# Turning k, q, v and the output of a gated delta rule by VectorE block transposes and DMA, with v's tile ahead of q's

## The chip, the cores and the metric

The kernel runs on one core of one Trainium2 chip. The metric is the device time of one launch in microseconds (us), the median of several runs. The core has five engines with queues of their own: TensorE (PE; its weight loads are listed as PEld), VectorE (DVE), ScalarE (ACT), GpSimd (POOL) and SyncE (SP), which here only issues DMAs. Sixteen DMA engines move the data.

## What is computed

The reference is one step of a decoder layer, in float32, for 512 new prompt tokens and 8 sample tokens of width 2048. The part that matters here is the gated delta rule of the prompt, with 8 heads of width 128. Its kernel form works on chunks of 128 tokens, four to a head.

```
xn  = rmsnorm(h);  proj = xn @ w_in            # q | k | v | z | beta | decay | pool
qkv = silu(short_conv(proj_qkv))               # 4 taps along the tokens
q, k = l2norm(q) * 128**-0.5, l2norm(k)
...
u  = solve(I + strict(k k^T * beta * decay), v * beta)     # and w, from k
qk = tril(q k^T * decay)
for each chunk:                                # the chain through the state S
    v_new = u - w S
    o = (q * exp(g)) S + qk v_new
    S = S * exp(g_last) + k_dec^T v_new
out = rmsnorm(o, dn_norm) * silu(z)
```

After that come a pooling group, the output projection, and a SwiGLU block, none of which the change touches.

## The kernel before, in words

All activations lie with channels on the 128 partitions and tokens along the free dimension: 8 sample columns and 512 prompt columns. A projection tile is 128 columns of the weights by all tokens. `product` (L172) makes it out of 16 k-steps, each of six matmuls (L168 to L170: two halves of the tokens, by three passes over the high and low parts of weights and activations). The weights come in granules of eight k-steps: SP loads `raw` (L131), ScalarE cuts off the high part (`hi`, L135), VectorE the rest (`lo`, L137), each in three buffers. These three carry a raised priority.

The stage of the change is the first one, up to L1163. For each half of the heads (0 to 3, then 4 to 7) the loop at L1101 makes the four k tiles, then four z tiles (L1111), then for each head the q tile and the v tile (`qv_tiles`, L1089). `qkv_tile` (L730) evicts the product into `ext` (L259, VectorE), runs four convolution steps (L737, L739) and SiLU on ScalarE (L740).

The delta rule's own small matmuls are woven into the products: `Weave` (L43) holds generators in two tracks, `product` calls `weave.step()` once per k-step, and a generator's `yield n` asks for n steps until its next piece. A task may be added with a delay in steps. TensorE's instructions stay in the order in which the program writes them (L522); those of the other engines and of SP are put in order by a scheduler that ranks ready instructions by their place in the program, raised for the weights and the evictions.

- `keys(h)` (L760) runs in track 1, 16 steps behind its k tile: k k^T (L766), the four transposes of k (L769) into PSUM, their squares on ScalarE (L757), the row factors, `nn` (L781) and the decayed keys `kd` (L783). The diagonal blocks of `nn` go through DRAM to `eliminate` (L794), 62 short VectorE instructions that invert them for four heads at a time; the result comes back as `utf` (L1093).
- `delta(h, qT, vT)` (L817) runs in track 0, from one step behind the second of the head's two tiles: the product with the inverse (L831), four transposes of q (L838) and their squares, two steps later L850 and the product of k and q (L857), then four transposes of v (L865) scaled into `vs` (L867), then the chain over the chunks (L877 to L896) with R and S on VectorE and W on ScalarE (L886). At its end squares of the output give row factors, and L910 writes the scaled output over `nn`.
- `gate(h)` (L913), in track 1, 8 steps later: four transposes of the output (L916), and one VectorE instruction that multiplies by the norm's weight and the gate into the mixed activations (L918), which are read again at L1140, behind the pool tiles.

What a transpose serves: k, q, v and the output exist with channels on partitions, while row factors and the chain want tokens there. A transpose is a TensorE instruction with the identity as one operand, and its result lies in PSUM.

## Time and profile before

| | |
|---|---|
| median of 3 runs | 2160.74 us (2160.28 to 2161.4) |
| the profiled execution | span 2158.9 us from first to last instruction |
| TensorE busy | 2136.1 us, 99% of the span |
| VectorE busy | 1746.4 us, 81% |
| ScalarE busy | 929.6 us, 43% |
| GpSimd busy | 433.8 us, 20% |
| DMA | 297.04 MB, queue of SP and ScalarE 36.3% of 16 engines |
| granted TensorE clock | 0.999 |

The profile comes from one execution; its times are those of that execution, while the median is of runs without one. A line such as `L865 PE MATMUL dn<-ident,vT 128*128 128x128 f32 x32 | 4.9, 274` is a group of instructions: line of the kernel, engine, operation, tile written and tiles read, shape, count, then busy us in total and mean ns of one. In a timeline a row begins with its start and its length in us; x4 says that four instructions are merged in it; the bracket at its end gives the engine's idle time ahead of it and what ended that. The lengths of matmuls overlap, as they are pipelined. Names of buffers carry numbers now and then, which mean nothing.

### The profile page before, as it was taken

What the parts mean: (1) busy time and instruction counts of PE and PEld (TensorE: products, weight loads), DVE (VectorE), ACT (ScalarE), POOL (GpSimd) and SP (SyncE); (2) the same over time, 40 slices, a digit from 0 to 9 for tenths busy, and PEclk for the clock granted to TensorE, in tenths of its full rate; (3) what the DMA queues carried; (4) which work ended last, traced back from release to release, by engine and by line L of the source; (5) the groups of instructions that cost most, each with busy time, mean ns of one, the idle gap of its engine ahead of it and who ended that gap; (6) DMA issues with size and microseconds to landing.
All of it is one profiled execution on the core that took longest, in us unless ns stands there. A gap on an engine that the chain in (4) does not pass through costs nothing.

```text
span 2158.9 us, 42980 instructions
## 1 busy us (share of the span) xinstructions
PE 2136.1 (99%) x17809; PEld 2128.8 (99%) x17809; DVE 1746.4 (81%) x2619; ACT 929.6 (43%) x1404; POOL 433.8 (20%) x512
## 2 busy tenths in 40 slices
PE   8999999999999999999999999999999999999998
PEld 7999999999999999999999999999999999999998
DVE  7786667666499979988988888888877898887997
ACT  6533443432264545434433434434334444435444
POOL 2210110111012202233233233232113302003100
PEclk9999999999999999999999999999999999999999
DMA  8343234323445543554554454454446746438343
GB/s 281 92 110 91 76 94 112 88 76 96 120 121 161 152 119 111 155 166 141 145 166 139 147 167 143 142 163 134 125 147 189 234 111 205 115 103 247 93 108 119
DMA packets 442497, 297.04 MB, mean 138 GB/s; under 512 B 26556, under 2 KB 423253, under 8 KB 438957
## 3 DMA queue, kind: packets, MB, share of 16 engines
q1 hardware_dynamic: 422733, 219.94, 36.3%
q0 software_dynamic: 18256, 73.55, 10.5%
q8 instruction: 139, 2.28, 0.5%
q10 hardware_dynamic: 1312, 0.80, 0.1%
q14 instruction: 57, 0.47, 0.1%
HBM read 251.47 MB, written 43.43 MB: 137 GB/s over the span
## 4 chain that ended last, share of the span: by engine, by line
PE 86%; DVE 8%; DMA 2%; issue 2%; ACT 1%; POOL 1%; SPq 0%; DVEq 0%; POOLq 0%; ACTq 0%
PE dn L1223 20%; PE dn L1222 20%; PE dn L1224 20%; PE mm L168 6%; PE mm L170 6%; PE mm L169 6%; DVE lo L1216 2%; DVE raw L1244 1%; PE dn L850 1%; DMA st<-a_d 1%; DVE lo L137 1%; POOL st L1776 0%; DMA xt<-in_x_prompt_dram 0%; PE dn L960 0%; PE dn L857 0%
## 5 line engine op out<-in xcount | busy, mean ns | idle before, releaser
L1215 ACT CAST hi<-raw 128x1024 fp32r<-128x1024 f32 (+1 forms) x422 | 427.4, 1027 | 400.2 <-DVE raw L1244 206.5
L1216 DVE TENSOR_TENSOR lo<-raw,hi 128x1024 fp32r<-128x1024 f32 (+1 forms) x422 | 527.4, 1270 | 87.1 <-ACT hi L1215 85.6
L168 PE MATMUL mm<-xh,hi 128*128 128x256 f32 (+1 forms) x1280 | 379.7, 297 | 2.4 <-DVE mixa L259 2.4
L169 PE MATMUL mm<-xl,hi 128*128 128x256 f32 (+1 forms) x1280 | 361.5, 282 | 0.9 <-DVE xl L350 0.7
L170 PE MATMUL mm<-xh,lo 128*128 128x256 f32 (+1 forms) x1280 | 361.8, 283 | 0.4 <-DVE lo L137 0.4
L168 PEld LDWEIGHTS mm<-xh,hi 128*128 128x128 f32 x1280 | 241.4, 189 | 3.7 <-DVE mixa L259 3.1
L169 PEld LDWEIGHTS mm<-xl,hi 128*128 128x128 f32 x1280 | 241.7, 189 | 1.7 <-DVE xl L350 1.7
L170 PEld LDWEIGHTS mm<-xh,lo 128*128 128x128 f32 x1280 | 240.8, 188 | 0.6 <-DVE lo L137 0.6
L1244 DVE TENSOR_TENSOR raw<-raw 128x1024 f32<-128x1024 f32 (+1 forms) x130 | 175.3, 1349 | 2.2
L1223 PE MATMUL dn<-b21l,hi 128*128 128x260 f32 x620 | 175.7, 283 | 0.4 <-DVE b21l L1786 0.4
L1224 PE MATMUL dn<-b21h,lo 128*128 128x260 f32 x620 | 175.4, 283 | 0.0
L1222 PE MATMUL dn<-b21h,hi 128*128 128x260 f32 x620 | 175.0, 282 | 0.0
L1224 PE MATMUL dn<-b11h,lo 128*128 128x260 f32 x612 | 173.4, 283 | 1.2 <-DVE lo L1216 1.1
L1223 PE MATMUL dn<-b11l,hi 128*128 128x260 f32 x612 | 173.3, 283 | 0.0
L1222 PE MATMUL dn<-b11h,hi 128*128 128x260 f32 x612 | 172.7, 282 | 0.0
L1222 PE MATMUL dn<-T1h,hi 128*128 128x260 f32 x556 | 158.1, 284 | 0.0
L1223 PE MATMUL dn<-T1l,hi 128*128 128x260 f32 x556 | 157.7, 284 | 0.0
L1224 PE MATMUL dn<-T1h,lo 128*128 128x260 f32 x556 | 156.7, 282 | 0.0
L1222 PE MATMUL dn<-B22h,hi 128*128 128x260 f32 x548 | 155.9, 284 | 0.0
L1223 PE MATMUL dn<-B22l,hi 128*128 128x260 f32 x548 | 155.6, 284 | 0.0
L1224 PE MATMUL dn<-B22h,lo 128*128 128x260 f32 x548 | 154.6, 282 | 0.4 <-DVE lo L1216 0.4
L135 ACT CAST hi<-raw 128x1024 fp32r<-128x1024 f32 (+2 forms) x86 | 87.1, 1014 | 148.2 <-PE mm L169 139.4
(659 smaller groups left out, 6422.5 us busy)
## 6 DMA issues: line engine op xcount, KB each, us to landing
raw<-in_w_gate_up_dram SPq DMA_DIRECT2D x134, 512.0 KB
raw<-in_w_in_dram SPq DMA_DIRECT2D x79, 512.0 KB
a_d<-mixa POOLq DMA_DIRECT2D x22, 1040.0 KB, 5.5
raw<-in_w_down_dram SPq DMA_DIRECT2D x48, 448.0 KB
mixb<-in_w_gate_up_dram SPq DMA_DIRECT2D x41, 512.0 KB
raw<-in_w_out_dram SPq DMA_DIRECT2D x25, 512.0 KB
st<-a_d POOLq DMA_DIRECT2D x49, 260.0 KB, 6.5
raw<-in_w_down_dram SPq DMA_DIRECT2D x24, 512.0 KB
```

Source lines behind the costliest of these rows:

```text
L135: act.copy(hi[:, r], raw[:, r])
L137: dve.tensor_tensor(lo[:, r], raw[:, r], hi[:, r].bitcast(F32), op=ALU.subtract)
L168: te.matmul(acc[ci], wh, hi[k][:, c0:c1], start=(k == 0), stop=False)
L169: te.matmul(acc[ci], wh, lo[k][:, c0:c1], start=False, stop=False)
L170: te.matmul(acc[ci], wl, hi[k][:, c0:c1], start=False, stop=(k == len(w) - 1))
L850: te.matmul(yp[0:96, c, j], xt_[:, c, :], udf[:, c, j] if it == 0 else v3(cur)[:, c, j], start=True, stop=True)
L1215: act.copy(hi, raw)
L1216: dve.tensor_tensor(lo, raw, hi.bitcast(F32), op=ALU.subtract)
L1222: te.matmul(acc, wh[:, k, :], xf[:, k, :], start=start and k == 0, stop=False)
L1223: te.matmul(acc, wh[:, k, :], xg[:, k, :], start=False, stop=False)
L1224: te.matmul(acc, wl[:, k, :], xf[:, k, :], start=False, stop=stop and k == wh.shape[1] - 1)
L1244: dve.tensor_tensor(r[name], r[a], r[b], op=op)
```

## The change

A helper `turn_blocks` takes the place of the sixteen TensorE transposes of a head. VectorE transposes each 32x32 block of a [128, 512] tile into `bt`, one DMA writes `bt` to DRAM in rows of 128 numbers, and four DMAs read it back, each for 32 partitions, in pieces of 32 numbers, so that the blocks come to their transposed places. All five are issued by SP.

```diff
 BUFS:
-    "vs": 1
+    "vs": 2, "bt": 2, "tq": 1

+        tok_d = dram.tile([4, H, NCH, P, P], F32, name="tok_d")
+
+        def turn_blocks(kind, h, src, dst):
+            bt = d1tile("bt", [P, SEQ], "bt")
+            dve.transpose(bt, src)
+            d = tok_d[kind, h]
+            sp.dma_start(d.rearrange("c p f -> p c f"), v3(bt))
+            rows = d.rearrange("c (i p) (j q) -> j p (c i) q", p=32, q=32)
+            for j in range(4):
+                sp.dma_start(dst[32 * j:32 * j + 32, :].rearrange("p (n q) -> p n q", q=32), rows[j])

 keys:
-            kd = kds[h] = d1tile("kd", [P, SEQ], "kd")
+            kd = kds[h]
-            ktp = pst()
-            for c in range(NCH):
-                te.transpose(ktp[:, ck(c)], kT[:, ck(c)], ident)
-            squares(ktp, ss)
+            squares(kd, ss)
-            dve.tensor_tensor(v3(kd), v3(ktp), bc3(ad), op=ALU.mult)
+            dve.tensor_tensor(v3(kd), v3(kd), bc3(ad), op=ALU.mult)

 delta:
-        def delta(h, qT, vT):
+        def delta(h, qT, qk, vs):
-            qtp = pst()
-            for c in range(NCH):
-                te.transpose(qtp[:, ck(c)], qT[:, ck(c)], ident)
-            squares(qtp, ss)
+            squares(qk, ss)
-                    vtp = pst()
-                    for c in range(NCH):
-                        te.transpose(vtp[:, ck(c)], vT[:, ck(c)], ident)
-                    vs = d1tile("vs", [P, SEQ], "vs")
-                    dve.tensor_tensor(v3(vs), v3(vtp), bc3(ik), op=ALU.mult)
+                    dve.tensor_tensor(v3(vs), v3(vs), bc3(ik), op=ALU.mult)
-            weave.add(gate(h, on), 1, 8)
+            turn_blocks(3, h, on, on)
+            weave.add(gate(h, on), 1, 12)

 gate:
-            otp = pst()
-            for c in range(NCH):
-                te.transpose(otp[:, ck(c)], on[:, ck(c)], ident)
+            dve.scalar_tensor_tensor(mix[h][:, NB:NTOK], on, dnw, mix[h][:, NB:NTOK], op0=ALU.mult, op1=ALU.mult)
             yield 1
-            dve.scalar_tensor_tensor(mix[h][:, NB:NTOK], otp, dnw, mix[h][:, NB:NTOK], op0=ALU.mult, op1=ALU.mult)

 qv_tiles:
+            vs = d1tile("vs", [P, SEQ], "vs")
+            qkv_tile(2, h, vs)
+            turn_blocks(2, h, vs, vs)
             qT = d1tile("s0", [P, SEQ], "qT")
             qkv_tile(0, h, qT)
-            vT = d1tile("s2", [P, SEQ], "vT")
-            qkv_tile(2, h, vT)
-            weave.add(delta(h, qT, vT), 0, 1)
+            qk = d1tile("tq", [P, SEQ], "qk")
+            turn_blocks(0, h, qT, qk)
+            weave.add(delta(h, qT, qk, vs), 0, 1)

 loop over the k tiles:
+                kds[h] = d1tile("kd", [P, SEQ], "kd")
+                turn_blocks(1, h, mixb[:, h % 4, 0:SEQ], kds[h])
                 weave.add(keys(h), 1, 16)

-    nc = _bacc.Bacc("TRN2", target_bir_lowering=False, num_devices=1)
+    nc = _bacc.Bacc("TRN2", target_bir_lowering=False, num_devices=1, dynamic_dma_scratch_size=8192)
```

The last line makes the area in which GpSimd's DMA descriptors are written smaller, which frees 8 KB on each partition; the added buffers (one more `vs`, two `bt`, one `tq`, of 2 KB each) take as much. For each head the v tile is now made ahead of the q tile.

## The prediction

> **What bounds the kernel now.** I read the page first, then the busy time by window, the groups of instructions, and the timelines of the three engines around one head.

> ```profile
> span 2158.9 us, 42980 instructions
> ...
> PE 2136.1 (99%) x17809; PEld 2128.8 (99%) x17809; DVE 1746.4 (81%) x2619; ACT 929.6 (43%) x1404; POOL 433.8 (20%) x512
> ```
> ```profile
> 160.00:330.00 170.00, 170.00 (x1472) 170.00 (x1471) 109.27 (x254) 79.05 (x174) 19.71 (x48) 1.00 0.33 87
> ...
> 390.00:530.00 140.00, 140.00 (x1216) 139.91 (x1215) 88.50 (x206) 50.51 (x122) 15.00 (x30) 1.00 0.31 82
> ```

> The second fence covers the two stretches in which heads 0 to 3 and 4 to 7 go through the delta rule; its columns are TensorE, its weight loads, VectorE, ScalarE, GpSimd, the granted clock and the DMA share. TensorE is busy in all of it, at full clock; VectorE for 109 of 170 us, the DMA engines for a third. TensorE's order is written out by hand, so what leaves its queue shortens the kernel, and whatever makes one of its instructions wait lengthens it by the same amount. The three runs have a median of 2160.7 us, the profiled execution a span of 2158.9 us; the 1.8 us around the span I leave as they are, and apply every change to both.

> **What TensorE loses: a gain.** One row stands for the groups of transposes; the four lines (L769, L838, L865, L916) have 32 each, 4 chunks for 8 heads.

> ```profile
> L838 PE MATMUL dn<-ident,qT 128*128 128x128 f32 x32 | 4.8, 272 | 0.0
> ```
> ```profile
> 161.90 1.03 PE L831 MATMUL dn<-utf,mixb 128*128 128x96 f32 x8
> 162.76 0.60 PE L838 MATMUL dn<-ident,qT 128*128 128x128 f32 x4
> 163.12 0.37 PE L168 MATMUL mm<-xh,hi 128*128 128x264 f32 x1
> ...
> 164.64 0.84 PE L850 MATMUL dn<-utf,xt__2137 128*96 128x96 f32 x8
> 165.32 1.08 PE L857 MATMUL dn<-qT,mixb 128*128 128x128 f32 x8
> ...
> 168.34 0.61 PE L865 MATMUL dn<-ident,vT 128*128 128x128 f32 x4
> 168.70 0.37 PE L168 MATMUL mm<-xh,hi 128*128 128x264 f32 x1
> ```

> Matmuls are pipelined, so the cost is the distance between starts, not the 272 ns: four transposes hold the queue from 162.76 to 163.12 and from 168.34 to 168.70, 0.36 us. 32 groups by 0.36 us are 11.5 us off the path, all of them in stretches where TensorE never idles.

> **What v ahead of q costs: a wait.** L857 multiplies kT by qT, and starts 3.4 us after the head's first delta matmul (L831 at 161.90). Before, q was the first of the two tiles and its qT long finished; the late one was vT, wanted only at 168.34. After, q is late, and L857 wants it. With one transpose group (L838) gone ahead of it, L857 is due at 165.32 - 0.36 = 164.96. When would qT be there? The tile that ends last passes the same work as v's did: eviction, four convolution steps, SiLU. Head 0, VectorE and then ScalarE:

> ```profile
> 160.29 0.42 DVE L259 TENSOR_TENSOR ext<-mm,rb 128x256 f32<-128x256 f32 x1 [0.28 <-PE mm L170]
> 160.75 0.50 DVE L737 TENSOR_SCALAR y<-ext,prm 128x512 f32<-128x512 f32 x1
> 161.30 1.23 DVE L137 TENSOR_TENSOR lo<-raw,hi 128x1024 fp32r<-128x1024 f32 x1
> 162.44 2.32 DVE L739 SCALAR_TENSOR_TENSOR y<-ext,prm,y 128x512 f32<-128x512 f32 x3
> ```
> ```profile
> 162.96 0.48 ACT L833 COPY xt__2137<-dn 128x384 f32<-128x384 f32 x1 [1.69 <-PE dn L831]
> 163.46 0.28 ACT L757 ACTIVATE junk<-dn 128x128 f32<-128x128 f32 x1
> ...
> 164.97 0.19 ACT L757 ACTIVATION_READ_ACCUMULATOR junk<-dn 128x1 f32 x1
> 165.19 1.28 ACT L740 ACT_TABLE_LOAD   x1
> 166.48 0.63 ACT L740 ACTIVATE vT<-y 128x512 f32<-128x512 f32 x1
> ```

> The convolution ends at 162.44 + 2.32 = 164.76, with a weight cut (L137) in its middle. The squares (L757) that stand ahead of SiLU now belong to q; after, they read the turned q and come behind SiLU, so the table load can begin at 163.44 and end at 164.72. SiLU then runs from 164.8 to 165.4 and L857 starts about 165.5: a wait of 0.5 us. Heads 1 to 3 and 5, 6 are different, for there the head before ends in the same moment:

> ```profile
> 192.29 0.69 DVE L910 TENSOR_TENSOR mixb<-dn,ro 128x512 f32<-128x512 f32 x1
> 192.90 0.41 DVE L259 TENSOR_TENSOR ext<-mm,rb 128x256 f32<-128x256 f32 x1
> 193.35 0.50 DVE L737 TENSOR_SCALAR y<-ext,prm 128x512 f32<-128x512 f32 x1
> 193.89 0.75 DVE L739 SCALAR_TENSOR_TENSOR y<-ext,prm,y 128x512 f32<-128x512 f32 x1
> 194.56 1.22 DVE L137 TENSOR_TENSOR lo<-raw,hi 128x1024 fp32r<-128x1024 f32 x1
> 195.69 1.53 DVE L739 SCALAR_TENSOR_TENSOR y<-ext,prm,y 128x512 f32<-128x512 f32 x2
> ```
> ```profile
> 197.05 1.08 PE L857 MATMUL dn<-qT,mixb 128*128 128x128 f32 x8
> ```

> The convolution ends at 197.22; with 0.63 us of SiLU and 0.1 us for two handovers qT is there at 197.95, and L857 is due at 197.05 - 0.36 = 196.69: 1.26 us. The change puts one instruction more into just this place: the block transpose of the output follows L910 (ready at 192.98), comes earlier in the program than the convolution, and the scheduler ranks by that. No row shows a block transpose. From below, a 128x512 VectorE instruction that reads one tensor takes 0.50 us (L737); from above I take the 1.23 us of L137, which has twice the columns. I choose 0.6, nearest to L737, with 0.05 of handover, as it also goes once through 512 columns. That makes 1.9 us a head. [...] Head 7 has the sample tokens' instructions on VectorE as well:

> ```profile
> 485.66 2.37 DVE L739 SCALAR_TENSOR_TENSOR y<-ext,prm,y 128x512 f32<-128x512 f32 x3
> ```
> ```profile
> 487.36 0.41 PE L857 MATMUL dn<-qT,mixb 128*128 128x128 f32 x2
> ```

> 488.03 + 0.73 against 487.00 is 1.76 us, with the block transpose 2.4. Together: 2 heads (0 and 4) by 0.5, 5 by 1.9, one by 2.4, that is 12.9 us; if the block transpose comes behind the convolution, 1.0 + 6.3 + 1.8 = 9.1; if it takes 1.23 us, six heads lose 0.6 more, 16.7. Behind the waiting L857 stands all of TensorE's queue, and nothing makes up for it.

> **The turns themselves.** Each of the 32 turns adds a block transpose and five DMAs on SP: 256 KB out in 512-byte runs, and four reads of 512 pieces of 128 bytes. The same pieces are in the trace (utf<-ud_d):

> ```profile
> q1 hardware_dynamic: 448, 0.11, 66.4%
> ```
> ```profile
> q1 hardware_dynamic: 29408, 14.62, 32.2%
> ```
> ```profile
> 153.55 2.55 SPq L1093 DMA_DIRECT2D utf<-ud_d  x5
> ```
> ```profile
> 114.47 0.53 SPq L797 DMA_DIRECT2D nb<-nd_d  x1
> ```
> ```profile
> 118.64 0.20 DVE L807 TENSOR_TENSOR tm<-nb,u 64x31 f32<-64x31 f32 x1 [0.30 <-DMA nb<-nd_d]
> ```

> The first row is the window 165.45 to 166.2, of whose packets most are short: 448 took 66.4% of 0.75 us, 0.5 us, so 2048 pieces take some 2.3 us. The second is the window 160 to 330: 29,408 packets in 54.7 us, so 512 long ones take 0.95 us. 3.2 us by 32 turns are 104 us of DMA time over the 450 us of the stage, on engines busy a third: room enough. SP issues in 0.51 us a piece, 160 issues. A DMA of 256 KB landed 4.1 us after its issue (114.47 to 118.6), so a turn takes 0.6 + 4.1 + 3 x 0.51 + 4.1, some 10.4 us, if SP is free. Who waits? SP's queue also carries the weights:

> ```profile
> SPq L131 <- DVE lo L137: 137.9, 32, 10.4
> ```
> ```profile
> ACT hi L135 <- DMA raw<-in_w_in_dram: 5.2, 1, 5.2
> ```

> Weight loads wait for free buffers (137.9 us in the window 160 to 530), and only once did a cut wait for a load; so I cost a few us of SP standing at a turn at nothing. If that cover were gone, each us of a late cut would be one us of TensorE. The turned v has a whole tile of q in between. The turned k of heads 3 and 7 stands ahead of the elimination; utf's loads are issued by 156.1 (153.55 + 2.55) and land about 160, the first delta matmul stands at 161.9, so up to 1.7 us of lateness are hidden there, and past that each us costs two, one for each half. The output's turn and its gate, four steps later, have no reader before the splits behind the pool tiles: nothing. [...]

> [...]

> **The sum.** -11.5 + 12.9 = +1.4 us: span 2160.3, time 2162.1 us.

> **The rivals.** *Forecast: what leaves TensorE's queue comes back as the wait of L857*, 2156 to 2166 by the bounds (9.1 to 16.7 us of waits). Chance 0.50.

> *Slower: the squares of the turned q land in the chain of chunks.* Before, they ran when nothing else pressed. After, qT + 10.4 us puts them beside the copies W and their users:

> ```profile
> 172.81 0.27 ACT L886 COPY W<-dn 128x128 f32<-128x128 f32 x1
> 176.92 0.27 ACT L886 COPY W<-dn 128x128 f32<-128x128 f32 x1 [3.84 <-PE dn L884]
> ```
> ```profile
> 174.04 0.38 PE L889 MATMUL dn<-W,kd 128*128 128x128 f32 x2
> ```

> W is ready at 173.08 and used at 174.04: 0.96 us to spare, while the four squares take 1.7 us (163.46 to 165.16). It decides from the point where they begin less than 1.7 us ahead of a W, or stand in ScalarE's order ahead of one and q lands later than the scheduler assumed. A burst that delays W by its 1.7 us costs 0.74; with 0.5 us of late landing 1.2 us a head, 9.6 in all: 2171.7 us. For it speaks that a turn may take longer behind SP's buffer waits (up to 10.4 us); against it, that W copies are 4 us apart, so that the burst has gaps. Chance 0.32.

> *Faster: the convolution of q gets VectorE to itself.* If the weight cut (1.2 us) and the output's block transpose come behind it, the waits shrink to 0 for heads 0 and 4, 0.1 for five, 0.6 for head 7, about 1.1 us: 2160.7 - 11.5 + 1.1 = 2150.3 us. Against it: the cut came in the middle in all rows. Chance 0.15.

> *Slow pieces.* [...] Chance 0.03. [...]

> **How the numbers follow.** A measurement of this kernel tells 0.2%, 4.3 us, from no change. The forecast's case is nearly all within it; the slower case and the slow pieces, with a little of the forecast's upper end in place of what the slower one has within the bound, give 0.34 slower; the faster case with 0.01 of the forecast's lower end 0.16. The range reaches from the faster case's upper half, 2151, to a little beyond the slower case, 2174; left out are the slow pieces and the outer halves of the two others, less than 0.2. The likeliest case by itself has 2156 to 2166.

> **What would show it.** Right: L857 idle before it, released by ScalarE's SiLU of qT, 0.5 us in heads 0 and 4, near 2 in the others, 13 us in all; no idle of TensorE for v, k or the output; weight cuts waiting for slots as now. Block transposes of 0.5 to 0.7 us. Wrong: L857 without idle (then 2150), TensorE idle for W with ScalarE at L757 (then 2172), or 128-byte reads of many us.

## The result, and the profile after

The changed kernel takes 2210.17 us (median of 4 runs, 2210.03 to 2211.22), the kernel before 2161.07 us beside it (2160.28 to 2163.34): 1.0228 times as long, 95% interval 1.0214 to 1.0243. The forecast was 2162.1 us with a range from 2151 to 2174. The profiled execution's span went from 2158.9 to 2209.5 us, 50.6 us longer.

The first lines of the page after:

```profile
span 2209.5 us, 43046 instructions
...
PE 2135.2 (97%) x17681; PEld 2125.7 (96%) x17681; DVE 1765.7 (80%) x2651; ACT 937.0 (42%) x1408; POOL 446.5 (20%) x512
```

TensorE has the 128 transposes less (17681 matmuls against 17809), yet it is busy for a smaller share of a longer span: it waits. The same two stretches by window as shown of before (TensorE, its loads, VectorE, ScalarE, GpSimd, granted clock, DMA share):

```profile
160.00:330.00 170.00, 143.78 (x1181) 142.65 (x1182) 105.47 (x244) 60.88 (x137) 18.43 (x33) 0.91 0.46 110
390.00:530.00 140.00, 121.61 (x1009) 120.32 (x1008) 93.96 (x214) 46.79 (x101) 15.81 (x24) 0.94 0.46 110
```

Before, TensorE was busy in every microsecond of both, at full clock. Now 26 and 18 us are idle, and the clock is no longer full. What TensorE waited for between 100 and 700 us (total, times, longest), after:

```profile
PE dn L840 <- DMA utf<-ud_d: 37.2, 2, 23.1
PE dn L863 <- ACT qT L740: 12.2, 6, 2.5
PE dn L960 <- DMA s<-in_state_delta_dram: 3.6, 1, 3.6
```

and before, in the same window, of these three nothing, but

```profile
PE mm L168 <- DVE mixa L259: 2.4, 3, 1.1
```

The second row after is the forecast's wait for qT. The first is the result: TensorE stands before the first delta matmul of head 0 and of head 4 (L831 before, L840 after) until the inverse has come back from the elimination.

The waits have a second price. Windows of the changed kernel just behind the two long waits, behind the wait for qT in head 3, and in undisturbed work:

```profile
180.20:185.00 4.80, 4.80 (x23) 4.80 (x24) 0.00 (x0) 0.48 (x1) 1.22 (x2) 0.50 0.20 30
427.90:434.20 6.30, 6.26 (x31) 6.29 (x32) 0.23 (x1) 2.09 (x9) 0.61 (x1) 0.50 0.44 69
286.50:291.00 4.50, 3.88 (x19) 3.88 (x20) 3.38 (x8) 1.85 (x2) 0.10 (x1) 0.62 0.81 194
209.00:213.00 4.00, 4.00 (x36) 4.00 (x35) 1.98 (x8) 2.13 (x7) 1.01 (x1) 1.00 0.85 180
```

At a granted clock of 0.50, 23 matmuls start in 4.8 us, and 36 in 4.0 us at full clock. Half of 4.8 and of 6.3 us is lost, 5.5 us; three stretches of 3.4 us (253.3, 287.4, 577.6) lose up to 1.7 us each, so that about 10 us are an upper estimate. The sum: -11.5 (transposes, as forecast) + 37.2 + 12.2 + 3.6 + 10 - 2.4 (the old waits of the z tiles, beside which the elimination no longer runs) = 49.1 of 50.6 us.

**Why the inverse is late** is read from SP's queue, in which the transfers ahead of the elimination stand: the row of decays to DRAM (gcr_d), its broadcasts (gcb), the diagonal blocks (nd_d) and their load (nb). Three rows before:

```profile
80.09 0.30 SPq L621 DMA_DIRECT2D gcr_d<-gr  x1
82.27 0.82 SPq L746 DMA_DIRECT2D gcb<-gcr_d  x2
86.23 0.38 SPq L131 DMA_DIRECT2D raw<-in_w_in_dram  x1
```

and after, the same place and then the end of the chain:

```profile
86.67 0.39 SPq L131 DMA_DIRECT2D raw<-in_w_in_dram  x1
87.11 0.47 SPq L621 DMA_DIRECT2D gcr_d<-gr  x1
87.67 1.94 SPq L753 DMA_DIRECT2D kd<-tok_d  x4
93.93 0.39 SPq L131 DMA_DIRECT2D raw<-in_w_in_dram  x1
94.36 0.58 SPq L758 DMA_DIRECT2D gcb<-gcr_d  x1
...
98.75 0.38 SPq L131 DMA_DIRECT2D raw<-in_w_in_dram  x1
99.88 3.32 SPq L753 DMA_DIRECT2D kd<-tok_d  x4
...
130.65 1.62 SPq L797 DMA_DIRECT2D nd_d<-mixb  x1
...
134.68 0.53 SPq L806 DMA_DIRECT2D nb<-nd_d  x1
```

Each weight load (raw) waits for a free buffer, and whatever stands behind it waits too: from 78 to 140 us SP waits seven times for the weight cut (`lo`, L137), 19.3 us in all, and the ten loads from 78.06 to 135.72 go 6.4 us apart on the average. The row of decays was ahead of the weight load at 86.23 and is now behind the one at 86.67; the first broadcast has slipped behind one more and goes at 94.36 instead of 82.27; nb goes at 134.68 instead of 114.47. Counted over SP's rows from the start, 17 weight loads stood ahead of nb before and 21 after. Four of them at 6.4 us are some 26 us, of the size of the 20.2 us by which nb is late. That the turned k itself wasn't what came last is read from VectorE. The squares of the last key run at 110.7 to 112.4 us, but its `nn`, at 109.80 before, comes at 127.70. Its decays (`dm`, made from gcb) are late, as their broadcast is issued only at 119.08, and VectorE waits for yet another broadcast ahead of it. Before and then after:

```profile
109.80 1.12 DVE L781 SCALAR_TENSOR_TENSOR mixb<-dn,sck,dm 128x128 f32<-128x128 f32 x4
```
```profile
123.84 1.13 DVE L761 SCALAR_TENSOR_TENSOR dm<-gcb,gcs,mneg 128x128 f32<-128x128 f32 x4
126.90 0.88 DVE L761 SCALAR_TENSOR_TENSOR dm<-gcb,gcs,mneg 128x128 f32<-128x128 f32 x3 [1.93 <-DMA gcb<-gcr_d]
127.70 1.12 DVE L790 SCALAR_TENSOR_TENSOR mixb<-dn,sck,dm 128x128 f32<-128x128 f32 x4
```

The elimination then takes 34.5 us instead of 27.9 (138.4 to 172.9, before 118.6 to 146.5), now beside the convolutions of v and q, so that utf's loads go 26 us later. When the inverse of head 0 has landed shows in GpSimd's copy of it, again before and after:

```profile
157.91 0.62 POOL L835 COPY uu<-utf 128x512 f32<-128x512 f32 x1 [3.54 <-DMA utf<-ud_d]
```
```profile
180.39 0.61 POOL L844 COPY uu<-utf 128x512 f32<-128x512 f32 x1 [2.39 <-DMA utf<-ud_d]
```

It is there 22 us later. Before, TensorE came to it at 161.9, so 4.0 us were covered; now TensorE is ready at 157.0, which uses that cover up, and waits 23.1 us, until 180.1.

### The profile page after: what moved, and what is told of

The parts are those of the page before. It is cut to its first block, busy times and chain, and to the rows that moved or that the text cites. A ratio compares the mean times of both kernels' runs of the same rounds, so it can differ in the third digit from the quotient of the medians.

```text
span 2209.5 us, 43046 instructions
## 1 busy us (share of the span) xinstructions
PE 2135.2 (97%) x17681; PEld 2125.7 (96%) x17681; DVE 1765.7 (80%) x2651; ACT 937.0 (42%) x1408; POOL 446.5 (20%) x512
## 4 chain that ended last, share of the span: by engine, by line
PE 84%; DVE 9%; DMA 2%; ACT 2%; issue 1%; POOL 0%; SPq 0%; DVEq 0%; ACTq 0%; POOLq 0%
PE dn L1227 21%; PE dn L1228 21%; PE dn L1229 21%; PE mm L168 5%; PE mm L170 5%; PE mm L169 5%; DVE lo L137 1%; DVE lo L1221 1%; DVE y L739 1%; DVE u L818 1%; DVE tm L816 1%; PE dn L856 1%; PE dn L863 0%; PE dn L960 0%; PE dn L778 0%
## 5 line engine op out<-in xcount | busy, mean ns | idle before, releaser
L168 PE MATMUL mm<-xh,hi 128*128 128x256 f32 (+1 forms) x1280 | 382.1, 299 | 0.2 <-DVE ccs L259 0.2
L170 PE MATMUL mm<-xh,lo 128*128 128x256 f32 (+1 forms) x1280 | 364.0, 284 | 0.4 <-DVE lo L137 0.4
L168 PEld LDWEIGHTS mm<-xh,hi 128*128 128x128 f32 x1280 | 243.9, 191 | 1.5 <-issue 0.9
L170 PEld LDWEIGHTS mm<-xh,lo 128*128 128x128 f32 x1280 | 242.9, 190 | 0.6 <-DVE lo L137 0.6
L1227 PE MATMUL dn<-b11h,hi 128*128 128x260 f32 x612 | 172.9, 282 | 0.0
L1413 POOL TENSOR_TENSOR mixa<-mixa 128x520 f32<-128x520 f32 x22 | 51.2, 2325 | 495.4 <-DVE mixa L1407 495.4
```

Of the source, the lines that this page charges most:

```text
L168: te.matmul(acc[ci], wh, hi[k][:, c0:c1], start=(k == 0), stop=False)
L170: te.matmul(acc[ci], wl, hi[k][:, c0:c1], start=False, stop=(k == len(w) - 1))
L1227: te.matmul(acc, wh[:, k, :], xf[:, k, :], start=start and k == 0, stop=False)
L1413: pool.tensor_tensor(q[:, 4:8:2, :], q[:, 1:4:2, :], q[:, 0:2, :], op=ALU.subtract)
```

## The experiments

Each is the changed kernel unless it says otherwise; line numbers shift by a few from kernel to kernel. Kernels that ran together share the runs of the kernel before, 2161.3 to 2161.6 us. Rows of waits are again TensorE's between 100 and 700 us.

**k_back: only k on TensorE again.**

```diff
-                kds[h] = d1tile("kd", [P, SEQ], "kd")
-                turn_blocks(1, h, mixb[:, h % 4, 0:SEQ], kds[h])
 keys:
-            kd = kds[h]
+            kd = kds[h] = d1tile("kd", [P, SEQ], "kd")
 ...
+            ktp = pst()
+            for c in range(NCH):
+                te.transpose(ktp[:, ck(c)], kT[:, ck(c)], ident)
-            squares(kd, ss)
+            squares(ktp, ss)
-            dve.tensor_tensor(v3(kd), v3(kd), bc3(ad), op=ALU.mult)
+            dve.tensor_tensor(v3(kd), v3(ktp), bc3(ad), op=ALU.mult)
```

> k is turned by TensorE again (four transposes of k in keys, no block transposes and no DMAs for k); q, v and the output stay turned by DMA, v's tile stays ahead of q's. Theory (k's turns make the elimination late, because their five DMAs a head and the writes of the diagonal blocks behind them stand in SP's one queue between weight loads that wait for slots): TensorE's waits for utf (37.2 us) and the half-clock stretches behind them go, the wait for qT stays at 12 to 14 us, 24 groups of transposes are still saved (8.6 us): 2161 - 8.6 + 13 = 2165 us, 2160 to 2170. Rival A (the turns of q, v and the output load VectorE and the DMA engines so that the elimination takes 34 us instead of 28 whatever k does): at least the second half's wait of 14 us stays, 2180 us or more.

Measured 2178.01 us (1.0077, 1.0062 to 1.0092).

```profile
PE dn L866 <- ACT qT L740: 13.1, 8, 2.5
PE dn L963 <- DMA s<-in_state_delta_dram: 3.5, 1, 3.5
```

No wait for utf is left, and nb is behind 17 weight loads again. So k's turns bring the long waits, and without them the wait for qT shows in all eight heads with the 13.1 us that the forecast had worked out as 12.9. The time is 8 us above the expected range and 13 above its middle: the wait for the state's load (3.5 us) stays, three half-clock stretches of 3.4 us cost up to 5 us, and some 4 us are not assigned.

**k_only: only k turned by DMA**, everything else as before the change (q's tile ahead of v's).

> Only k is turned by DMA; q, v and the output are turned by TensorE, and q's tile is ahead of v's as before. Theory: both waits for utf stay, about 23 and 14 us, with the half clock behind them, and no wait for qT: 2161 - 2.9 + 37 + 5 to 10 = 2195 to 2206 us. Rival A (the other turns' load): in the second half, where the turns of q, v and the output of the first half run beside the k tiles, the wait shrinks to a few us: 2180 to 2190 us.

Measured 2181.59 us (1.0094, 1.0077 to 1.0111).

```profile
PE dn L840 <- DMA utf<-ud_d: 24.0, 2, 21.6
```

The first half's wait is k's alone (21.6 us; 21 weight loads ahead of nb). In the second half only 2.4 us are left, so there the rival held. The second half's 14 us need both: with k's turns alone they are 2.4 us, with the turns of q, v and the output alone (k_back) there is no wait, and in the changed kernel all of them stand on SP.

**k_dead: the turn of k without a reader.** As k_back, but the block transpose and the five DMAs are still issued.

```diff
-                kds[h] = d1tile("kd", [P, SEQ], "kd")
-                turn_blocks(1, h, mixb[:, h % 4, 0:SEQ], kds[h])
+                dead = d1tile("tq", [P, SEQ], "dead")
+                turn_blocks(1, h, mixb[:, h % 4, 0:SEQ], dead)
```

> k is turned by TensorE for the computation, but its block transpose and the five DMAs are still issued for each head, into a tile that nobody reads. Theory in its strong form (SP's queue is what is late: the DMAs push the broadcasts of the decay and the writes of the diagonal blocks back whether or not anybody needs the turned k): the elimination still begins 8 to 20 us late and TensorE waits for utf 10 to 30 us: 2180 to 2200 us. Rival B (only the dependence matters: the squares of the turned k, and nn and the elimination behind them, wait for a turn of 20 us, and the crowding of SP costs nothing): no wait for utf, within 3 us of the kernel with k turned by TensorE and without these DMAs.

Measured 2208.63 us (1.0222, 1.0204 to 1.024).

```profile
PE dn L843 <- DMA utf<-ud_d: 30.1, 2, 24.7
```

30.1 us of waits, against 37.2, come although nobody needs the turned k; the time is above the theory's range, whose waits were 10 to 30 us. So the dependence on the turned k, on which the forecast had thought (1.7 us of cover, then double), isn't needed for the loss; what is late are the other transfers of the chain. The two figures can't simply be taken from one another, as SP's order is not the same here: 22 weight loads stand ahead of nb.

**k_ready: five DMAs a head that wait for no engine.** As k_back, with this at the place of k's turn:

```diff
+                dead = d1tile("tq", [P, SEQ], "dead")
+                sp.dma_start(tok_d[1, h].rearrange("c p f -> p c f"),
+                             win_view(1024 + h * P)[:, 0:NCH, :])
+                rows = w_in[0, 0:SEQ, h * P:h * P + P].rearrange("(c i p) (j q) -> j p (c i) q", c=NCH, p=32, q=32)
+                for j in range(4):
+                    sp.dma_start(dead[32 * j:32 * j + 32, :].rearrange("p (n q) -> p n q", q=32), rows[j])
```

> k on TensorE, q, v and the output turned by SP's DMAs, and for each head five more DMAs on SP at the place of k's turn that wait for no engine: a copy of 256 KB of a weight into DRAM in 512-byte runs and four reads of 512 pieces of 128 bytes of a weight into a tile that nobody reads. Beside the kernel with dead turns of k (2208.6 us) it has the same number of issues and about the same bytes, but no block transpose to wait for and no write that has to land before the reads. Theory F (SP stands at each write for the block transpose and at each read for the landed write, and all behind it waits): within 7 us of the kernel without these DMAs, 2175 to 2185 us. Rival E (the issues themselves, 0.5 us each, and the pieces fill SP and the DMA engines): the waits for utf come back, 2195 to 2210 us.

Measured 2208.31 us (1.022, 1.0206 to 1.0233).

```profile
PE dn L843 <- DMA utf<-ud_d: 26.8, 2, 16.5
```

Theory F fell: SP's own standing at the turn, which I had costed at nothing in the forecast and then suspected, is not what is needed; DMAs that wait for no engine do it as well (20 weight loads ahead of nb). By the waits of its queue SP stood at two of them, 2.5 us before 70 us and 1.4 us (for ScalarE) after 200, but at none from 70 to 200 us, where the first nb falls behind. The numbers of rival E came out, but its reason is at most a part: between 86.7 and 129.0 us the issues of the added DMAs take 6.8 us of SP, while nb is 14.7 us later than in k_back. That the DMA engines are not full either (a share of 0.52 from 100 to 160 us in the changed kernel) is shown by the next kernel.

**all_pool: all turns on GpSimd's queue.**

```diff
+            on_q = pool if kind in (0, 1, 2, 3) else sp
-            sp.dma_start(d.rearrange("c p f -> p c f"), v3(bt))
+            on_q.dma_start(d.rearrange("c p f -> p c f"), v3(bt))
 ...
-                sp.dma_start(dst[32 * j:32 * j + 32, :].rearrange("p (n q) -> p n q", q=32), rows[j])
+                on_q.dma_start(dst[32 * j:32 * j + 32, :].rearrange("p (n q) -> p n q", q=32), rows[j])
```

> The changed kernel, with all 160 DMAs of the turns issued by GpSimd's queue instead of SP's; same bytes, same 128-byte pieces, same order of the work. Theory (place in SP's queue): SP's loads, the broadcasts and the diagonal blocks are no longer held up, the waits for utf fall from 37.2 us to under 5 and the wait for the state's load (3.6 us) goes, the wait for qT stays at 12 to 13 us with some 5 us of half clock: 2161 - 11.5 + 13 + 5 = 2168 us, 2160 to 2180; if GpSimd takes long to write the descriptors, its own powers come late and the sum is at the upper end or above. Rival C (the latency of the transfers and the 128-byte pieces themselves): waits for utf stay over 25 us, 2195 us or more.

Measured 2169.26 us (1.0035, 1.0022 to 1.0048), 41 us less than the changed kernel with the same work, the same bytes and the same 128-byte pieces.

```profile
PE dn L864 <- ACT qT L740: 8.8, 7, 1.7
...
PE dn L841 <- DMA utf<-ud_d: 2.0, 1, 2.0
```

The waits for utf fall from 37.2 to 2.0 us, and the state's load is no longer waited for. GpSimd's rows of head 3's turn:

```profile
95.71 0.77 POOL L751 DMA_DIRECT2D tok_d<-bt  x1 [0.57 <-DVE bt L748]
...
99.28 2.60 POOL L754 DMA_DIRECT2D kd<-tok_d  x4 [2.56 <-DMA tok_d<-bt]
```

From the block transpose at 94.7 to the last read's issue at 101.9 the turn takes 7 us, about 10 with the landing (3.0 us for the write, 4.0 for the reads), as the forecast had it for a free queue. GpSimd's issue of a read takes 0.65 us (median), SP's in the changed kernel 0.49. On SP, in the changed kernel, the same turn has its block transpose at 89.6 and the last read's issue at 103.2. Bandwidth was not measured here; another queue was worth 41 us, by what stands in it ahead and behind.

**k_act: k's turns on ScalarE's queue**, the others on SP.

> The changed kernel, with the five DMAs of each turn of k issued by ScalarE's queue; q, v and the output stay on SP. Theory: the first half's wait for utf (23 us), which k's turns alone make, falls to under 5 us; the second half's (14 us), which with k alone turned was 2.4 us and so comes mostly from the turns of q, v and the output on SP, stays at 5 to 14: 2180 to 2195 us, plus what ScalarE's cuts lose while ScalarE stands at a write or a read. Rival C: both stay, 2205 us or more.

Measured 2214.57 us (1.0243, 1.0228 to 1.0258), with 35.1 us of waits for utf: the theory missed, and rival C's number came out. SP's part now was on time (first broadcasts at 85.0), but ScalarE's instructions stand in a fixed order too, with weight cuts that wait for TensorE (48 times between 60 and 560 us, 100.7 us in all):

```profile
101.88 1.03 ACT L135 CAST hi<-raw 128x1024 fp32r<-128x1024 f32 x1
103.56 1.97 ACTq L754 DMA_DIRECT2D kd<-tok_d  x3
...
114.07 0.31 ACT L770 ACTIVATE junk<-kd 128x128 f32<-128x128 f32 x1
```

The last three reads of head 3 went only at 103.6, behind a cut, and squares of k stood at 114 to 117 us, where nn of the last key before the change had already been at 109.8. A queue paced by the weights is no better for being another one.

**k_prio: k's turn with the raised priority of the weight loads.**

```diff
+                with tc.high_priority(offset=AHEAD):
-                turn_blocks(1, h, mixb[:, h % 4, 0:SEQ], kds[h])
+                    turn_blocks(1, h, mixb[:, h % 4, 0:SEQ], kds[h])
```

> The changed kernel as it is, but the block transpose of k and its five DMAs get the raised priority that the weight loads have, so that they stand further ahead in VectorE's and SP's orders; nothing else is moved. Theory: the turned k of head 3 lands some 8 to 10 us after its SiLU instead of 20, the elimination begins earlier by about that, the two waits for utf shrink from 37 us to 10 to 25: 2185 to 2200 us, unless SP, now standing at the writes and reads, makes weight cuts late (each us one us). Rival C (the turn's own latency and its 128-byte pieces, not its place in the queue, make k late): utf waits stay over 30 us, within 5 us of the changed kernel (2210).

Measured 2212.54 us (1.0238, 1.0222 to 1.0253), again with 37.2 us of waits for utf. The rival's number came out, not the theory's, but the rival's reason failed: the turn of head 3 was early (reads issued at 92.8 instead of 99.9). But the first broadcast now went at 99.2, later than in the changed kernel.

**chain_prio: the other way round**, the raised priority for gcr_d, gcb, nd_d and nb.

> The changed kernel with the same four kinds of small transfers left on SP, but with the raised priority of the weight loads, so that the scheduler can put them ahead of weight loads; the added DMAs and their issue times are all still on SP. Theory G: the waits for utf fall to 5 to 20 us, 2180 to 2195 us, unless SP then stands at a block that is not computed yet and a weight load comes late. Rival E (issue time and transfers of the added DMAs fill SP): waits for utf over 30 us, 2203 us or more.

Measured 2218.04 us (1.0265, 1.0251 to 1.0279), with 37.7 us of waits for utf: rival E's number. Now the broadcasts are early (first at 82.8), and k's turn is what comes last: head 3's write at 109.2, its last read at 121.8. In both of these orders on SP whatever comes second ends up behind the weight loads; others were not tried.

**chain_pool: the small transfers of the chain on GpSimd, all turns on SP.**

```diff
-            sp.dma_start(gcr_d, gr)
+            pool.dma_start(gcr_d, gr)
-            sp.dma_start(gcb, gcr_d[h:h + 1, :].broadcast_to([P, SEQ]))
+            pool.dma_start(gcb, gcr_d[h:h + 1, :].broadcast_to([P, SEQ]))
```

and so for nd_d and nb.

> The changed kernel with all turns on SP; only the small transfers of the elimination's chain (the row of decays to DRAM, its broadcasts, the writes of the diagonal blocks, the load of them for the elimination) are issued by GpSimd instead. Theory G (these fell behind further weight loads in SP's fixed order): the 37.2 us of waits for utf fall to 5 to 18, what is left being the turned k's own lateness (its squares at 110.7 us against the nn of the last key at 109.8 before, and the same again in the second half): 2180 to 2192 us. Rival H (it is the turned k itself, held up on SP, that is late): waits for utf over 25 us, 2198 us or more.

Measured 2199.84 us (1.0177, 1.0161 to 1.0192).

```profile
PE mm L168 <- DVE mixa L259: 10.4, 5, 4.9
PE dn L840 <- DMA utf<-ud_d: 9.9, 2, 7.1
```

The waits for utf fall from 37.2 to 9.9 us, in the middle of what theory G gave: 27 us were these small transfers' place on SP, and at most 10 the turned k itself. The time is still 8 us above the expected range. Two things were not in it: the first row, 10.4 us where the changed kernel has none, and half clock, seven stretches of 30.7 us in all, which cost up to 14 us, some 3 more than in the changed kernel. For the first row, VectorE stands at the head of the second elimination, and the evictions of the z tiles are behind it in its order.

```profile
370.33 0.20 DVE L816 TENSOR_TENSOR tm<-nb,u 64x31 f32<-64x31 f32 x1 [5.95 <-DMA nb<-nd_d]
```

**k_back_d4, all_pool_d4, all_pool_d4_y3: the delta rule begun later.** In the first two the task starts 4 steps behind the q tile instead of 1, on top of k_back and of all_pool; the third also gives three steps instead of two between its first and second product.

```diff
-            weave.add(delta(h, qT, qk, vs), 0, 1)
+            weave.add(delta(h, qT, qk, vs), 0, 4)
```

> The kernel with k on TensorE and q, v and the output turned by DMA (2178 us), with the delta rule of each head begun 4 steps behind its q tile instead of 1, so 3 steps of 0.72 us, 2.2 us, later. Theory: the wait of L857's successor for qT (13.1 us) falls to 0 to 3 us and the half-clock stretches that follow the long ones go: 2178 - 11 to 13 - 3 to 5 = 2160 to 2164 us. Rival D (the delta rule's chain then ends later, and the next head's first matmuls or the state's load wait instead): 2170 us or more.

> All turns on GpSimd's queue, and the delta rule of each head begun 4 steps behind the q tile instead of 1. Theory: the waits for qT (8.8 us) and utf (2.0 us) and half of the half-clock stretches go; against that the delta rule's second product now waits some 0.5 us in six heads for ScalarE's copy, as it did with k on TensorE: 2169.3 - 10.8 - 1.7 + 3 = 2159.8 us, 2156 to 2163. Rival D (the later chain moves the waits to the next head or to the state's load): 2165 us or more.

> As the kernel with all turns on GpSimd's queue and a delay of 4 steps, with three steps instead of two between the delta rule's first product and its second, so that ScalarE's copy has time. Theory: the 0.5 us waits of six heads go, 3 us less than with two steps: 2154 to 2159 us, faster than both kernels. Rival: the chain, one step longer, makes the next head's work wait as much as it saves, no difference to two steps.

Measured 2169.13 (1.0034, 1.0022 to 1.0046), 2168.2 (1.0031, 1.0019 to 1.0043) and 2163.61 us (1.001, 1.0001 to 1.0019), each above its expected range. The wait for qT is gone in the first and is 1.7 us in the second, so the delay covers it, but other waits take its place: in k_back_d4 six waits of 0.5 to 1.6 us for ScalarE's copy xt_ (4.1 us), 1.9 us for S, 4.9 for the state's load. One more step took 4.6 us off, more than the 3 expected, and the kernel is still not below the one before. Rival D held in part.

**kqo_pool: q's tile first again, k, q and the output on GpSimd's queue, v on TensorE.**

> k, q and the output turned by DMAs on GpSimd's queue, v on TensorE, and q's tile ahead of v's as before. Theory: no wait for qT without any delay, as q is a tile earlier, 24 groups of transposes saved (8.6 us), a wait for utf of 2 us and a half-clock stretch (1.7 us) as with all turns on GpSimd: 2161.3 - 8.6 + 2 + 1.7 + 2 = 2158 us, 2154 to 2162. Rival (turned q on GpSimd's queue delays its powers and copies in the chain): W or R waits of 0.5 us and more a head, 2163 us or more.

Measured 2163.26 us (1.0007, 0.9999 to 1.0016): no difference that can be told, and 1 us above the expected range.

```profile
PE mm L168 <- DVE mixa L259: 5.7, 4, 3.4
PE dn L841 <- DMA utf<-ud_d: 4.7, 1, 4.7
```

Without a wait for qT, the 8.6 us of transposes are given back by k's turn, even on a free queue: 4.7 us for utf, 3.3 more at the z tiles, and the half clock behind them, up to 5. The rival's waits for W or R don't show. The kernel with q and the output alone, below, has none of these.

**o_only: only the output turned, on SP.**

> Only the output is turned by block transposes and DMA; k, q and v on TensorE, q's tile ahead of v's. Theory: 8 groups of transposes saved, 2.9 us; no wait for utf or qT; the state's load behind the last turns may still cost 3.5 us: 2157 to 2163 us. Rival A (the output's turns crowd SP in the second half's k tiles): a wait for utf of 3 us or more in the second half, 2164 us or more.

Measured 2165.82 us (1.0018, 1.0008 to 1.0028), above the expected range, though without a wait for utf.

```profile
PE dn L970 <- DMA s<-in_state_delta_dram: 3.6, 1, 3.6
```

The output's turn, costed at nothing, isn't free on SP either: the sample tokens' state load comes late behind it, 3.6 us and a half-clock stretch of 6.8 us, against 2.9 us of transposes.

**qo_pool: q and the output turned on GpSimd's queue, k and v on TensorE, q's tile first.**

> Only q and the output are turned by DMA, on GpSimd's queue; k and v on TensorE, q's tile ahead of v's. From the ledger: 16 groups of transposes saved (5.8 us), no wait for qT, utf as before (the last key's chain is untouched), a wait of 0.6 us in a head or two for ScalarE's copy: 2161.5 - 5.8 + 1 = 2156.7 us, 2154 to 2160, faster than both kernels by a little over 0.2%. Rival (GpSimd's issues delay its own copies and powers, VectorE's block transposes delay the evictions of the z tiles): 2160 us or more, no difference that can be told.

Measured 2154.71 us (2154.34 to 2155.25) against 2161.57: 0.9969, 0.9958 to 0.9981, faster than both kernels.

```profile
PE 2128.9 (99%) x17745; PEld 2121.7 (99%) x17745; DVE 1757.6 (82%) x2635; ACT 929.4 (43%) x1404; POOL 493.7 (23%) x592
```
```profile
160.00:330.00 170.00, 170.00 (x1468) 170.00 (x1467) 114.96 (x267) 79.54 (x177) 49.29 (x88) 1.00 0.43 112
390.00:530.00 140.00, 140.00 (x1213) 140.00 (x1211) 95.04 (x214) 51.39 (x123) 39.59 (x65) 1.00 0.41 108
```

TensorE is busy throughout both stretches again, at full clock, and the 64 transposes less show whole: 16 groups of 0.36 us are 5.8 us, and the span is 2152.7 us, 6.2 us shorter. These are the two turns whose result is wanted late and on which no elimination waits.

## Why the prediction was wrong, step by step

**The transposes: right.** 0.36 us a group is what leaves TensorE; qo_pool shows it for 16 groups, without new waits.

**The wait for qT: right.** 12.2 us in six heads against 12.9; heads 0 and 4, which had been given 0.5 us each, are covered by the wait for utf, and in k_back all eight give 13.1. The order on VectorE was the one forecast, the output's block transpose and a weight cut ahead of the convolution's steps (L739):

```profile
212.86 0.70 DVE L748 STREAM_TRANSPOSE bt<-mixb 128x512 f32<-128x512 f32 x1
213.49 1.18 DVE L137 TENSOR_TENSOR lo<-raw,hi 128x1024 fp32r<-128x1024 f32 x1
...
215.10 2.33 DVE L739 SCALAR_TENSOR_TENSOR y<-ext,prm,y 128x512 f32<-128x512 f32 x3
```

What was left out is the clock behind such waits, up to 5 us in k_back (one of its three stretches is behind the state's load). One bound was added up wrongly: 9.1 us of waits give 2158.3 us, not 2156; nothing hangs on it.

**The block transpose: right in size.**

```profile
L748 DVE STREAM_TRANSPOSE bt<-mixb 128x512 f32<-128x512 f32 x16 | 11.3, 706 | 2.8 <-ACT mixb L740 2.8
```

0.71 us against 0.6, within 0.50 to 1.23.

**The turn's length, 10.4 us, right for a free queue (all_pool); its place in the queue: the step that failed.** The prediction put it so: weight loads wait for free buffers, "so I cost a few us of SP standing at a turn at nothing". It looked at the cover of the weight cuts, and that cover held: in this stage TensorE waited for no late cut. But the same queue carries the transfers ahead of the elimination, and these have little cover: the prediction had read off 1.7 us, and head 0's inverse was there 4.0 us early. It asked only whether the turned k would be late by itself, and didn't ask what else of the chain is queued beside the turn on SP. Put behind four more weight loads in the first half and three more in the second (51 against 48 ahead of the second nb), that cost TensorE 23 us of waiting in the first and 14 in the second: 37.2 us, and with the clock about 43, where the forecast had 0. k_dead, k_ready, chain_pool and all_pool show it from four sides; chain_pool, which moves nothing but these transfers, takes 27 us of it away. That the scheduler's ranking placed these transfers so is read from SP's order; why it ranked them so was not tried apart.

**The output's turn: wrong by 3.6 us**, the state's load behind it on SP; all_pool and qo_pool do without it. **The smaller descriptor area:** no cost shows; qo_pool has it, and is faster. It was not tried by itself.

**The rivals.** The slower one named a collision of ScalarE's squares with W; TensorE never waited for W in the changed kernel. It had the direction right, not the mechanism. The faster one: the cut and the block transpose came ahead of the convolution, not behind. Slow pieces: no run shows 128-byte reads that are slow; all_pool has them at 3.3 us from issue to landing (median; 6.0 the longest), and takes 7.7 us more than the kernel before.

## What to carry to other kernels

A DMA added to a queue that also carries loads paced by buffers is paid for by what it pushes back: list every transfer on that queue whose result lies on a short-cover chain, and count how many paced loads stand ahead of each before and after (17 against 21 here), which the scheduled order of the program should tell before a run. Put added transfers on a queue with no paced instructions (here GpSimd's; ScalarE's, with its cuts, was no better), and turn only what is wanted late. A long TensorE idle cost 2.4 and 3.1 us here beyond itself in half clock.

## What was not expected of the hardware

The granted clock fell behind waits much shorter than the long ones, and not behind all of them. Two waits for qT in the changed kernel, in heads 3 and 7:

```profile
287.12 1.82 PE L863 MATMUL dn<-qT,mixb 128*128 128x128 f32 x8 [1.92 <-ACT qT L740]
...
534.48 1.16 PE L863 MATMUL dn<-qT,mixb 128*128 128x128 f32 x8 [2.46 <-ACT qT L740]
```

After 1.92 us of idle the window 286.5 to 291 has 0.62 (shown above); after 2.46 us the clock stays full. The stretches at half clock in this trace, 3.413, 17.07 and 23.89 us, are 1, 5 and 7 times 3.413 us. Their starts (161.1, 253.3, 287.4, 417.1 and 577.6 us) also lie on one grid, 27, 10, 38 and 47 steps of 3.413 us apart; a window is one such step in what follows. On this grid the two waits differ:

```profile
284.02:287.44 3.42, 1.50 (x15) 1.34 (x14) 3.08 (x6) 0.98 (x2) 0.10 (x1) 1.00 0.79 205
...
529.78:533.20 3.42, 2.23 (x21) 2.07 (x20) 3.35 (x6) 1.03 (x4) 1.30 (x3) 1.00 0.29 70
533.20:536.61 3.41, 2.13 (x18) 2.13 (x19) 3.18 (x8) 0.63 (x1) 0.87 (x3) 1.00 0.89 241
```
